# Two SwiGLU FFNs with seven block products for gate and up, a grouped down projection, and three modulation vectors made during the short convolution

## The chip, the core and the metric

One core of one Trainium2 chip runs the whole program. The metric is the device time of one execution in microseconds (us), as a median of several runs. The engines of the core work side by side, each through its own queue, strictly in the order of that queue: TensorE (PE, matrix products), VectorE (DVE, elementwise work), ScalarE (ACT, activations and copies), GpSimd (POOL, elementwise work too) and SyncE (SP, which here issues the transfers from HBM). An instruction whose inputs or whose output buffer are not ready holds up everything behind it in its own queue.

## The reference, cut to what matters

The program is two layers of a diffusion backbone on 512 tokens of 1024 channels: an attention and state-space mixer with a SwiGLU FFN behind it, then a short-convolution mixer with a second FFN, then a last normalisation. The part that the change rewrites is the FFN, and the modulation around it:

```python
D_MODEL = 1024; SEQ = 512
FFN_HIDDEN = -(-(8 * D_MODEL) // (3 * 256)) * 256      # 2816 = 22 blocks of 128

def modulate(h, shift, scale):
    return h * (1 + scale) + shift

def swiglu(h, w_gate, w_up, w_down):
    return (jax.nn.silu(h @ w_gate) * (h @ w_up)) @ w_down
```

For each layer a 1024 x 6144 matrix (`ada`) times a conditioning vector gives six modulation vectors of 1024: shift, scale and gate of the mixer (parts 0, 1, 2) and shift, scale and gate of the FFN (parts 3, 4, 5).

## The kernel before, in words

**Layout.** Activations lie transposed: 128 channels on the partitions, tokens along the free dimension. The residual stream is `xT`, eight blocks (`d` or `k`, 0 to 7) of 128 channels by 512 tokens. The tokens are handled in two halves of 256, called `e=0` and `e=1`.

**Precision.** A float32 product is made of three products of rounded operands (`mm3`, lines 113 to 118): hi times hi, hi times lo, lo times hi. So every weight block of 128x1024 is fetched into `wst` (DMA, L108), rounded by ACT into `whi` (L94), and DVE makes the rest `wlo = wst - whi` (L95). There are three buffers of each; `take` (from line 97) gives the next block of the list `plan` and starts the fetch of the ones ahead of it. Activations have a hi and a lo half in the same way (`act_hi`, `act_lo`).

**FFN before.** For each of the 22 hidden blocks `f` PE makes gate and up: two blocks of weights, eight channel blocks each, three products, 48 matmuls of 128x128 on 512 tokens. `finish` puts silu (ACT, L979), the product of gate and up (DVE, L980) and the split in hi and lo (L94, L95) behind it. All 22 hidden blocks stay in memory. Then `project` makes the down projection: for each of the eight output blocks 22 x 3 matmuls, and DVE adds the gated result to `xT` (L916). The last output block is done in two token halves, so that the norm of the first half can start while PE still works on the second.

**Norms.** The sum of squares gathers in `sq_acc` (ACT squares, POOL adds, L325). `renorm` is a job that waits on a list `due` and is called on as PE's program grows: ones-matmuls sum over the partitions (L333), nine small DVE steps make the reciprocal root (L142 to L150), a matmul spreads it over the partitions (L307), and `entry` makes the next stage's activations from it, block by block: DVE multiplies (L945), ACT or DVE applies scale and shift (L947, L949), ACT rounds (L951), DVE or POOL makes the lo half (L952). `renorm` yields 3500 columns of PE work before L333 and 8500 before L307; `flush` runs such jobs out at once. `together` (L961, L963) is the first product of a stage, made half by half.

**Modulation.** `ada_rest` fetches one 128x512 block of `ada` after the other (`ada_st`, L251), and DVE multiplies it by the conditioning vector and adds it up (L255 for the first of eight, L257 for the rest); after eight steps a transpose and a reduction follow (L260, L261). It is called in steps by `pump`. Before, part 5 of layer 0 and all six of layer 1, 7 x 16 = 112 steps, run in FFN 0 with four buffers of `ada_st`.

**Order.** The PE queue has the order in which the code is written. A scheduler orders the queues of the other engines, and the order that it chose is fixed when the program is built.

Of the kernel before, what the change touches and what calls it, by code (L numbers as in the profile page):

```python
# [7 lines left out]
F32 = mybir.dt.float32  # L8
# [31 lines left out]
NCON = CAT[-1]  # L40

# [12 lines left out]

def halves(ap):
    return ap.rearrange("p (a b) -> p a b", a=2)


class Block:
    def __init__(self, ctx, tc, t):  # L60
# [3 lines left out]
        self.plan, self.ready, self.used = [], [], 0  # L64
# [31 lines left out]

    def take(self, ahead=2):
        n = self.used
        self.used += 1
        for i in range(len(self.ready), min(n + ahead + 1, len(self.plan))):  # L100
            self.ready.append(self.weight(*self.plan[i]))
        w, self.ready[n] = self.ready[n], None
        return w

    def weight(self, src, n, extra=False):
# [3 lines left out]
        hi, lo = ((self.np if extra else self.wp).tile([P, 1024], F32R, name=x, tag=x, bufs=1 if extra else 3)  # L109
                  for x in ("whi", "wlo"))  # L110
        self.split(hi[:, :n], lo[:, :n], st[:, :n])
        return hi, lo
# [123 lines left out]
    def ada_rest(self, pool, layer, parts, acc=None, bufs=2, tag=None):  # L236
# [3 lines left out]
        for n, part in enumerate(parts):  # L240
            for j in range(2):
# [4 lines left out]
                for k in range(0, KC, step):  # L246
                    if acc is None:
# [91 lines left out]
    def hybrid(self):  # L339
# [5 lines left out]
        with tc.tile_pool(name="start", bufs=1) as sp:  # L345
# [22 lines left out]
            def weights():  # L368
                for i in range(3):
                    self.ready.append(self.weight(*self.plan[i]))  # L370
# [526 lines left out]
    def project(self, xt, m, gate, between, nk=KC, order=None, tail=1, lead=0, more=True):  # L897
# [32 lines left out]
        ws = [load(2 + more - i) for i in range(tail)]  # L930
# [6 lines left out]
    def entry(self, xt, i, j):  # L937
        nc = self.nc
        gsc, sh = self.gsc[:, i, j, :], self.mod[:, i, 3 * j, :]

        def run(e, rb):
            ts = slice(TC * e, TC * e + TC)
            for k in range(KC):
                u = self.np.tile([P, TC], F32, name="nm_u", tag="nm_u", bufs=3)
                nc.vector.tensor_tensor(u, xt[:, k, ts], rb, ALU.mult)  # L945
                if k % 2:
                    nc.vector.tensor_scalar(u, u, gsc[:, k:k + 1], sh[:, k:k + 1], ALU.mult, ALU.add)  # L947
                else:
# [193 lines left out]
```

## Time and profile before

| what | value |
|---|---|
| median of 3 runs (lowest to highest) | 1294.58 us (1290.67 to 1295.09) |
| the profiled execution: its time, its span | 1294.68 us, 1292.9 us |
| PE busy | 1241.5 us, 96% of the span |
| DVE, ACT, POOL busy | 731.7, 448.0, 182.7 us |
| the span by stages, roughly | mixer of layer 0 to 345 us, FFN 0 to 735, short convolution to 907, FFN 1 to 1281, last norm to the end |

The profiled execution lasts 1.8 us longer than its span, and lies 0.1 us above the median. A row of the trace gives a start in us, a duration, the engine, the line, the operation, and what it writes and reads; in brackets stands how long the engine had been idle before it and what ended that idle time.

### The profile page before, as it was taken

What the parts mean: (1) busy time and instruction counts of PE and PEld (TensorE: products, weight loads), DVE (VectorE), ACT (ScalarE), POOL (GpSimd) and SP (SyncE); (2) the same over time, 40 slices, a digit from 0 to 9 for tenths busy, and PEclk for the clock granted to TensorE, in tenths of its full rate; (3) what the DMA queues carried; (4) which work ended last, traced back from release to release, by engine and by line L of the source; (5) the groups of instructions that cost most, each with busy time, mean ns of one, the idle gap of its engine ahead of it and who ended that gap; (6) DMA issues with size and microseconds to landing.
All of it is one profiled execution on the core that took longest, in us unless ns stands there. A gap on an engine that the chain in (4) does not pass through costs nothing.

```text
span 1292.9 us, 15877 instructions
## 1 busy us (share of the span) xinstructions
PE 1241.5 (96%) x6086; PEld 1022.4 (79%) x6086; DVE 731.7 (57%) x1187; ACT 448.0 (35%) x675; POOL 182.7 (14%) x199
## 2 busy tenths in 40 slices
PE   5999988899999999999999999999999999999997
PEld 3887665567798888888888988888988888888886
DVE  4898899976464777788522564443643333332223
ACT  4534534455353222222222342223532222222221
POOL 3433435440220000000000110002200000000001
PEclk9998989999999999999999999999999999999998
DMA  9331453300413777777433323333133333333322
GB/s 370 125 98 49 123 166 119 98 1 1 149 63 122 229 250 241 226 235 255 123 102 90 115 67 97 98 98 114 50 114 98 98 98 98 92 96 90 92 88 66
DMA packets 54845, 158.52 MB, mean 123 GB/s; under 512 B 6000, under 2 KB 8688, under 8 KB 54512
## 3 DMA queue, kind: packets, MB, share of 16 engines
q1 hardware_dynamic: 54480, 157.20, 38.3%
q8 instruction: 48, 0.79, 0.3%
q10 hardware_dynamic: 288, 0.31, 0.1%
q14 instruction: 29, 0.24, 0.1%
HBM read 154.86 MB, written 2.10 MB: 121 GB/s over the span
## 4 chain that ended last, share of the span: by engine, by line
PE 83%; DVE 9%; issue 3%; DMA 3%; POOL 1%; ACT 1%; SPq 0%; DVEq 0%; ACTq 0%; POOLq 0%
PE psS L116 14%; PE psS L117 14%; PE psS L118 14%; PE psA L116 10%; PE psA L118 10%; PE psA L117 10%; PE psV L830 2%; DMA adaw<-ada 2%; PE psS L961 1%; DVE xtok L257 1%; DVE mx L804 1%; PE psS L822 1%; DVE wlo L95 1%; PE psS L963 1%; DMA xT<-xT 1%
## 5 line engine op out<-in xcount | busy, mean ns | idle before, releaser
L95 DVE TENSOR_TENSOR wlo<-wst,whi 128x1024 fp32r<-128x1024 f32 (+2 forms) x194 | 234.9, 1214 | 317.2 <-ACT whi L94 311.8
L94 ACT CAST whi<-wst 128x1024 fp32r<-128x1024 f32 (+2 forms) x194 | 198.4, 1026 | 549.9 <-PE psS L117 258.5
L116 PE MATMUL psS<-act_hi,whi 128*128 128x512 f32 x760 | 297.5, 391 | 1.0 <-DVE cs_a L573 0.9
L118 PE MATMUL psS<-act_hi,wlo 128*128 128x512 f32 x760 | 297.2, 391 | 0.0
L117 PE MATMUL psS<-act_lo,whi 128*128 128x512 f32 x760 | 297.2, 391 | 0.0
L118 PEld LDWEIGHTS psS<-act_hi,wlo 128*128 128x128 f32 x760 | 143.3, 189 | 30.0
L116 PEld LDWEIGHTS psS<-act_hi,whi 128*128 128x128 f32 x760 | 143.2, 188 | 29.3 <-issue 1.2
L117 PEld LDWEIGHTS psS<-act_lo,whi 128*128 128x128 f32 x760 | 143.2, 188 | 27.7
L325 POOL TENSOR_TENSOR sq_acc<-sq_acc,sq 128x512 f32<-128x512 f32 (+1 forms) x28 | 38.0, 1356 | 872.2 <-issue 645.7
L116 PE MATMUL psA<-ffn_h_hi,whi 128*128 128x512 f32 (+1 forms) x396 | 145.4, 367 | 0.0
L117 PE MATMUL psA<-ffn_h_lo,whi 128*128 128x512 f32 (+1 forms) x396 | 145.0, 366 | 0.0
L118 PE MATMUL psA<-ffn_h_hi,wlo 128*128 128x512 f32 (+1 forms) x396 | 145.0, 366 | 0.0
L257 DVE SCALAR_TENSOR_TENSOR ada_acc<-ada_st,silu_c,ada_acc 128x512 f32<-128x512 f32 x98 | 73.5, 750 | 25.5 <-DMA ada_st<-ada 24.0
L117 PEld LDWEIGHTS psA<-ffn_h_lo,whi 128*128 128x128 f32 x396 | 74.7, 189 | 12.0
L118 PEld LDWEIGHTS psA<-ffn_h_hi,wlo 128*128 128x128 f32 x396 | 74.7, 189 | 12.1
L116 PEld LDWEIGHTS psA<-ffn_h_hi,whi 128*128 128x128 f32 x396 | 74.7, 189 | 11.9
L116 PE MATMUL psA<-act_hi,whi 128*128 128x512 f32 (+1 forms) x216 | 80.0, 370 | 0.1
L118 PE MATMUL psA<-act_hi,wlo 128*128 128x512 f32 (+1 forms) x216 | 79.2, 367 | 0.8 <-DVE wlo L95 0.8
L117 PE MATMUL psA<-act_lo,whi 128*128 128x512 f32 (+1 forms) x216 | 79.6, 368 | 0.0
L916 DVE SCALAR_TENSOR_TENSOR xT<-psA,mod,xT 128x512 f32<-128x512 f32 (+1 forms) x40 | 25.6, 643 | 67.9 <-PE psA L118 67.7
L94 ACT CAST ffn_h_hi<-sg 128x512 fp32r<-128x512 f32 x44 | 27.3, 621 | 59.0 <-DVE sg L980 59.0
L118 PEld LDWEIGHTS psA<-act_hi,wlo 128*128 128x128 f32 x216 | 40.8, 189 | 8.1 <-DVE wlo L95 1.3
(297 smaller groups left out, 1810.7 us busy)
## 6 DMA issues: line engine op xcount, KB each, us to landing
wst<-w_gu SPq DMA_DIRECT2D x88, 512.0 KB, 3.6
ada_st<-ada SPq DMA_DIRECT2D x112, 256.0 KB, 4.0
wst<-w_dn SPq DMA_DIRECT2D x32, 512.0 KB, 3.5
wst<-ada SPq DMA_DIRECT2D x24, 512.0 KB, 3.8
wst<-w_sc SPq DMA_DIRECT2D x24, 512.0 KB, 3.7
adaw<-ada SPq DMA_DIRECT2D x16, 512.0 KB, 10.4
wst<-w_dn SPq DMA_DIRECT2D x16, 384.0 KB, 3.2
wst<-w_f SPq DMA_DIRECT2D x10, 512.0 KB, 3.6
```

Of the source, the lines that this page charges most:

```text
L94: nc.scalar.copy(hi, src)
L95: nc.vector.tensor_tensor(lo, src, hi.bitcast(F32), ALU.subtract)
L116: nc.tensor.matmul(out, lhsT=a[0], rhs=b[0], start=start, stop=False)
L117: nc.tensor.matmul(out, lhsT=a[0], rhs=b[1], start=False, stop=False)
L118: nc.tensor.matmul(out, lhsT=a[1], rhs=b[0], start=False, stop=stop)
L257: nc.vector.scalar_tensor_tensor(a, w[:, i], c, a, ALU.mult, ALU.add)
L325: nc.gpsimd.tensor_tensor(self.acc[:, ts], self.acc[:, ts], sq, ALU.add)
L804: nc.vector.tensor_reduce(mx[:, c:c + 1], s[:, 0:768], AX.X, ALU.max)
L822: nc.tensor.matmul(s[:, a * T:a * T + T], lhsT=kt[x][:, ks], rhs=q[x], start=(x == 0), stop=(x == 1))
L830: nc.tensor.matmul(av, lhsT=vz[:, kc, vs], rhs=e[:, a], start=(c + a == 0), stop=(c + a == CHUNKS - 1))
L916: nc.vector.scalar_tensor_tensor(xt[:, d, ts], ps, gate[:, d:d + 1], xt[:, d, ts], ALU.mult, ALU.add)
L961: nc.tensor.matmul(out, lhsT=a[:, k * P:(k + 1) * P], rhs=hi, start=(k == 0 and a is w[0]), stop=False)
```

## The change

**Gate and up by seven products.** The 2x2 block product (gate and up weights, each cut in two halves of four channel blocks, times activations cut in two channel halves and two token halves) is made with seven block products in place of eight, by sums and differences of the blocks. Each of the seven is 4 x 3 matmuls on 256 tokens: 84 matmuls for an `f`. They come in three steps per `f`: A (two products), B (three), C (two). The activation sums `t1` to `t4` are made in `combine`, part of the entry of `e=1`. The weight sums are made for each `f`: four additions of 128x512 on POOL, whose results are rounded again by ACT and DVE. The products are put together by DVE (L1175) in the tile `seven`. The lo half of the hidden block moves from DVE to POOL (L1212).

**Grouped down projection.** The hidden blocks come in groups of 5, 5, 4, 4, 4. After a group is done, its part of all eight output blocks is made and added to `xT` (L1115); only the last group of four goes through `project`.

**Modulation.** FFN 0 makes four parts (64 steps), the short convolution makes parts 3, 4, 5 of layer 1 (48 steps). `ada_st` has two buffers in place of four, and the sum is kept in the tile `u_first`.

**Weights ahead.** `take` and `release` hand over weight buffers by a count of large and small pieces; an extra buffer pair for the first block of a stage is dropped.

```diff
+SEVEN = (0, 1)
+GROUPS = ((0, 5), (5, 10), (10, 14), (14, 18), (18, 22))
+QUARTERS = 4
+
+def steps():
+    out = [("A", 0), ("A", 1), ("A", 2), None]
+    for f in range(NF):
+        out += [("A", f)] * (f > 2) + [("B", f), ("C", f)]
+        out += [("D", g) for g in range(len(GROUPS) - 1) if GROUPS[g][1] == f]
+    return out
...
+    def prepare(self, raw, i, kind, f):
+        nc, t = self.nc, self.t
+        if kind == "D":
+            return [self.down(i, d, f) for d in range(KC)]
+
+        def first():
+            st = raw[f] = self.wp.tile([P, 1024], F32, name="wst", tag="wst", bufs=3)
+            nc.sync.dma_start(out=st, in_=t["w_gu"][i, f, 0])
+            return self.rounded(self.wp, "whi", "wlo", 3, st)
+
+        def sums():
+            a1, a2 = raw[f], self.sv.tile([P, 1024], F32, name="wsu", tag="wsu", bufs=2)
+            nc.sync.dma_start(out=a2, in_=t["w_gu"][i, f, 1])
+            h = slice(0, 512), slice(512, 1024)
+            st = self.sv.tile([P, 1024], F32, name="wsa", tag="wsa", bufs=1)
+            s3, s4 = (self.sv.tile([P, 512], F32, name=x, tag=x, bufs=n) for x, n in (("ws3", 1), ("ws4", 2)))
+            nc.gpsimd.tensor_tensor(st[:, h[1]], a2[:, h[0]], a2[:, h[1]], ALU.add)
+            nc.gpsimd.tensor_tensor(st[:, h[0]], st[:, h[1]], a1[:, h[0]], ALU.subtract)
+            nc.gpsimd.tensor_tensor(s3, a1[:, h[0]], a2[:, h[0]], ALU.subtract)
+            nc.gpsimd.tensor_tensor(s4, a1[:, h[1]], st[:, h[0]], ALU.subtract)
+            raw[f] = s3, s4, a2[:, h[1]]
+            return self.rounded(self.wp, "whi", "wlo", 3, st)
+
+        def small(x):
+            return lambda: self.rounded(self.sv, "qhi", "qlo", QUARTERS, raw[f][x])
+
+        return {"A": [first], "B": [sums, small(0)], "C": [small(1), small(2)]}[kind]
...
+            if seven and e:
+                return combine(rb)
...
+        def combine(rb):
+            for k in range(4):
+                u = []
+                for x in (k, k + 4):
+                    u.append(self.np.tile([P, TC], F32, name="nm_u", tag="nm_u", bufs=3))
+                    nc.vector.tensor_tensor(u[-1], xt[:, x, TC:], rb, ALU.mult)
+                    affine(u[-1], x, nc.scalar)
+                t1, t4 = self.u0[:, k], self.u0[:, k + 4]
+                t2 = self.np.tile([P, TC], F32, name="nm_t", tag="nm_t", bufs=2)
+                nc.vector.tensor_tensor(t1, u[0], t1, ALU.subtract)
+                nc.vector.tensor_tensor(t2, u[1], t1, ALU.subtract)
+                split(self.sums(0, k), t2, nc.vector)
+                split(self.act.at(k, 1), t1, nc.vector)
+                nc.gpsimd.tensor_tensor(u[0], u[1], u[0], ALU.subtract)
+                split(self.sums(1, k), u[0], nc.gpsimd)
+                split(self.act.at(k + 4, 1), u[1], nc.vector)
+                nc.gpsimd.tensor_tensor(t4, t4, t2, ALU.subtract)
+                split(self.sums(2, k), t4, nc.gpsimd)
...
     def ffn(self, i, xt, after, bg=None):
...
+            def down(g):
+                for d in range(KC):
+                    w = self.take()
+                    ps = self.psA()
+                    lo, hi = GROUPS[g]
+                    for k in range(lo, hi):
+                        c = slice((k - lo) * P, (k - lo + 1) * P)
+                        self.mm3(ps, [a[:, c] for a in w], hid.at(k), k == lo, k == hi - 1)
+                    nc.vector.scalar_tensor_tensor(xt[:, d], ps, gate[:, d:d + 1], xt[:, d], ALU.mult, ALU.add)
+                    self.pump(1)
+
+            (self.gated_seven if i in SEVEN else self.gated)(fp, hid, down)
+            lo, hi = GROUPS[-1]
+            self.project(xt, Shifted(hid, lo), gate, after, hi - lo, lead=3 * (i in SEVEN), more=(i == 0))
...
+    def gated_seven(self, fp, hid, down):
...
+            if kind == "A":
+                p = self.get()
+                ps = self.psA((P, 2, TC))
+                cs = fp.tile([P, 4, TC], F32, name="seven", tag="seven", bufs=3)
+                product(ps[:, 0], half(p, 0), b11)
+                nc.scalar.copy(cs[:, 2], ps[:, 0])
+                product(ps[:, 1], half(p, 1), b21)
+                add(cs[:, 0], ps[:, 1], cs[:, 2])
+                live[f] = cs
+            elif kind == "B":
+                cs = live[f]
+                ps = self.psS().rearrange("p (a b) -> p a b", a=4)
+                p, q = self.get(), self.get()
+                product(ps[:, 0], half(p, 0), t2)
+                add(cs[:, 2], ps[:, 0], cs[:, 2])
+                product(ps[:, 2], q, t3)
+                add(cs[:, 3], ps[:, 2], cs[:, 2])
+                product(ps[:, 1], half(p, 1), t1)
+                z = ps[:, 1]
+                add(cs[:, 1:3], z[:, None].broadcast_to([P, 2, TC]), cs[:, 2:4])
+            else:
+                cs = live.pop(f)
+                ps = self.psA((P, 2, TC))
+                p, q = self.get(), self.get()
+                product(ps[:, 0], p, b22)
+                product(ps[:, 1], q, t4)
+                add(cs[:, 1:4:2], ps, cs[:, 1:4:2])
+                g = cs[:, 0:2]
+                nc.scalar.activation(g, g, AF.Silu)
+                for e in range(2):
+                    nc.vector.tensor_tensor(g[:, e], g[:, e], cs[:, 3 - e], ALU.mult)
+                hi, lo = hid.new(f)
+                nc.scalar.copy(hi, g)
+                nc.gpsimd.tensor_tensor(lo, g, hi.bitcast(F32), ALU.subtract)
...
+        self.flush(1)
+        for n, x in enumerate(steps()):
+            if x is None:
+                self.flush()
+            elif x[0] == "D":
+                down(x[1])
+            else:
+                step(*x)
+                if n > 3:
+                    self.pump(2 if x[1] < 6 and x[0] != "B" else 1)
...
     def shortconv(self, xt, after):
         nc, tc, t = self.nc, self.tc, self.t
         with tc.tile_pool(name="sconv", bufs=1) as fp:
             m = Pair(fp, "sconv_h", KC)
+            acc = [self.u0[:, x:x + 2].rearrange("p a b -> p (a b)") for x in (4, 6)]
+            self.queue.append(self.ada_rest(fp, 1, (3, 4, 5), acc, bufs=2, tag="ada_st"))
             self.flush(1)
...
                 self.split(*m.at(j), halves(acc))
+                self.pump(7)
+            self.pump(1000)
             self.project(xt, m, self.mod[:, 1, 2, :], after, tail=3)
...
             def late(fp):
-                yield from self.ada_rest(fp, 0, (5,), bufs=4, tag="sg")
-                yield from self.ada_rest(fp, 1, range(6), bufs=4, tag="sg")
+                acc = [self.u0[:, x:x + 2].rearrange("p a b -> p (a b)") for x in (0, 2)]
+                yield from self.ada_rest(fp, 0, (5,), acc, bufs=2, tag="ada_st")
+                yield from self.ada_rest(fp, 1, range(3), acc, bufs=2, tag="ada_st")
```

The order of instructions on the engines other than PE is the scheduler's, so the diff does not tell it. Three places are shown. In each row stand the line, the operation, the written and the read tiles and the shape.

DVE at the start of FFN 0, before: the last entry rows of `e=1`, the first product of gate and up (`sg`), and the next weight roundings.

```order
L945 TENSOR_TENSOR nm_u<-xT,psA 128x256
L952 TENSOR_TENSOR act_lo<-nm_u,act_hi 128x256
L945 TENSOR_TENSOR nm_u<-xT,psA 128x256
L947 TENSOR_SCALAR nm_u<-nm_u,gsc,mod 128x256
L952 TENSOR_TENSOR act_lo<-nm_u,act_hi 128x256
L980 TENSOR_TENSOR sg<-sg,psS 128x512
L95 TENSOR_TENSOR wlo<-wst,whi 128x1024 x2
```

The same place after the change: the end of `combine` (`nm_u`, `nm_t`, `u_first` are u, t2 and t1/t4; `tsum` holds the rounded sums), where the last row is the first addition of step B.

```order
L1052 TENSOR_TENSOR tsum_lo<-nm_t,tsum_hi 128x256
L1074 TENSOR_TENSOR u_first<-nm_u,u_first 128x256
L360 SCALAR_TENSOR_TENSOR u_first<-ada_st,silu_c,u_first 128x512
L1070 TENSOR_TENSOR nm_u<-xT,psA 128x256
L1052 TENSOR_TENSOR act_lo<-u_first,act_hi 128x256
L360 SCALAR_TENSOR_TENSOR u_first<-ada_st,silu_c,u_first 128x512
L1075 TENSOR_TENSOR nm_t<-nm_u,u_first 128x256
L1052 TENSOR_TENSOR act_lo<-nm_u,act_hi 128x256
L360 SCALAR_TENSOR_TENSOR u_first<-ada_st,silu_c,u_first 128x512
L1052 TENSOR_TENSOR tsum_lo<-nm_t,tsum_hi 128x256
L360 SCALAR_TENSOR_TENSOR u_first<-ada_st,silu_c,u_first 128x512
L1175 TENSOR_TENSOR seven<-psS,seven 128x256
```

Modulation steps (L358, L360) now stand between the steps of the entry: eight of them between the first rows of `combine` and that addition, where before there was none until the entry was over.

DVE at the start of the short convolution, before: the reciprocal root of `e=0` and the first rows of its entry.

```order
L142 TENSOR_SCALAR rs_v<-psV 128x2
L143 TENSOR_SCALAR rs_y<-rs_v 128x2
L144 TENSOR_TENSOR rs_t<-rs_y 128x2
L145 SCALAR_TENSOR_TENSOR rs_t<-rs_t,rs_v 128x2
L146 SCALAR_TENSOR_TENSOR rs_y<-rs_t,rs_y 128x2
L147 TENSOR_TENSOR rs_t<-rs_y 128x2
L148 SCALAR_TENSOR_TENSOR rs_q<-rs_t,rs_v 128x2
L149 SCALAR_TENSOR_TENSOR rs_t<-rs_q 128x2
L150 SCALAR_TENSOR_TENSOR rs_y<-rs_t,rs_y 128x2
L95 TENSOR_TENSOR wlo<-wst,whi 128x1024
L945 TENSOR_TENSOR nm_u<-xT,psA 128x256 x3
```

After, the same chain of nine and the first rows of the entry:

```order
L248 SCALAR_TENSOR_TENSOR rs_t<-rs_t,rs_v 128x2
L358 TENSOR_SCALAR u_first<-ada_st,silu_c 128x512
L249 SCALAR_TENSOR_TENSOR rs_y<-rs_t,rs_y 128x2
L250 TENSOR_TENSOR rs_t<-rs_y 128x2
L360 SCALAR_TENSOR_TENSOR u_first<-ada_st,silu_c,u_first 128x512
L251 SCALAR_TENSOR_TENSOR rs_q<-rs_t,rs_v 128x2
L252 SCALAR_TENSOR_TENSOR rs_t<-rs_q 128x2
L253 SCALAR_TENSOR_TENSOR rs_y<-rs_t,rs_y 128x2
L360 SCALAR_TENSOR_TENSOR u_first<-ada_st,silu_c,u_first 128x512
L1060 TENSOR_TENSOR nm_u<-xT,psA 128x256 x3
```

Three modulation steps stand inside the chain. In all, 23 of them (two groups of eight with their transposes and reductions, and seven more) stand ahead of the first weight rounding for the second block, `j=1`:

```order
L364 TENSOR_REDUCE ada_red<-u_first 128x16
L358 TENSOR_SCALAR u_first<-ada_st,silu_c 128x512
L360 SCALAR_TENSOR_TENSOR u_first<-ada_st,silu_c,u_first 128x512 x5
L1246 TENSOR_TENSOR u_first<-u_first,psA 128x512
L360 SCALAR_TENSOR_TENSOR u_first<-ada_st,silu_c,u_first 128x512
L180 TENSOR_TENSOR wlo<-wst,whi 128x1024
```

The transfer queue SP at the same place, before (24 weight blocks of the short convolution, then those of its output projection):

```order
L108 DMA wst<-w_sc 128x1024 x24
L108 DMA wst<-w_so 128x1024 x8
```

After, the weights and the blocks of `ada` share it:

```order
L212 DMA wst<-w_sc 128x1024 x5
L354 DMA ada_st<-ada 128x512 x2
L212 DMA wst<-w_sc 128x1024
L354 DMA ada_st<-ada 128x512 x23
L212 DMA wst<-w_sc 128x1024
```

The buffers `ada_st` of the short convolution lie in memory that FFN 0 used, and the first of these transfers waits for the last matmul of FFN 0's down projection.

## Rows read from the trace of the kernel before

**Rows 1.** The page: busy time of each engine; the chain that ended last, by engine.
```profile
PE 1241.5 (96%) x6086; PEld 1022.4 (79%) x6086; DVE 731.7 (57%) x1187; ACT 448.0 (35%) x675; POOL 182.7 (14%) x199
...
PE 83%; DVE 9%; issue 3%; DMA 3%; POOL 1%; ACT 1%; SPq 0%; DVEq 0%; ACTq 0%; POOLq 0%
```
**Rows 2.** Busy time by stretches; columns in the second row, PEclk the granted clock.
```profile
core 0: us, PE busy (x) PEld busy (x) DVE busy (x) ACT busy (x) POOL busy (x), PEclk, DMA share, GB/s
395.00:615.00 220.00, 220.00 (x973) 182.27 (x972) 162.81 (x219) 65.71 (x82) 0.00 (x0) 1.00 0.71 229
715.00:745.00 30.00, 28.39 (x224) 27.43 (x223) 17.50 (x43) 12.13 (x21) 5.61 (x5) 1.00 0.34 106
910.00:945.00 35.00, 34.45 (x249) 32.27 (x248) 25.88 (x57) 19.62 (x37) 8.12 (x10) 1.00 0.26 77
...
1284.00:1286.00 2.00, 0.91 (x4) 0.91 (x4) 0.87 (x6) 0.00 (x0) 0.00 (x0) 0.50 0.15 50
```
**Rows 3.** Timeline of PE, matmuls on 256 tokens; from the first to the last 22 steps.
```profile
718.35 0.28 PE L118 MATMUL psA<-ffn_h_hi,wlo 128*128 128x256 f32 x1
...
720.99 0.28 PE L116 MATMUL psA<-ffn_h_hi,whi 128*128 128x256 f32 x1
```
**Rows 4.** Timeline of DVE in FFN 0; then the transfers of `ada_st` from 395 to 700.
```profile
453.46 0.75 DVE L257 SCALAR_TENSOR_TENSOR ada_acc<-ada_st,silu_c,ada_acc 128x512 f32<-128x512 f32 x1 [0.21 <-DMA ada_st<-ada]
454.13 0.69 DVE L95 TENSOR_TENSOR ffn_h_lo<-sg,ffn_h_hi 128x512 fp32r<-128x512 f32 x1
454.73 0.75 DVE L257 SCALAR_TENSOR_TENSOR ada_acc<-ada_st,silu_c,ada_acc 128x512 f32<-128x512 f32 x1
457.48 0.75 DVE L257 SCALAR_TENSOR_TENSOR ada_acc<-ada_st,silu_c,ada_acc 128x512 f32<-128x512 f32 x1 [2.00 <-DMA ada_st<-ada]
...
  DMA ada_st<-ada: 24.0, 21
DMA to landing us min/median/max: 2.8/4.0/5.6
```
**Rows 5.** Timelines of DVE and POOL: alone, and beside each other.
```profile
358.09 0.73 POOL L325 TENSOR_TENSOR sq_acc<-sq_acc,sq 128x256 f32<-128x256 f32 x1 [2.15 <-ACT sq L322]
364.62 1.23 DVE L95 TENSOR_TENSOR wlo<-wst,whi 128x1024 fp32r<-128x1024 f32 x1
364.99 1.46 POOL L325 TENSOR_TENSOR sq_acc<-sq_acc,sq 128x256 f32<-128x256 f32 x1 [6.16 <-ACT sq L322]
365.76 0.70 DVE L150 SCALAR_TENSOR_TENSOR rs_y<-rs_t,rs_y 128x2 f32<-128x2 f32 x1
378.13 0.16 DVE L150 SCALAR_TENSOR_TENSOR rs_y<-rs_t,rs_y 128x2 f32<-128x2 f32 x1
719.94 1.29 POOL L325 TENSOR_TENSOR sq_acc<-sq_acc,sq 128x512 f32<-128x512 f32 x1 [13.67 <-ACT sq L322]
```
**Rows 6.** The entry of `e=1` in FFN 0 on DVE: first and last two rows.
```profile
379.17 1.08 DVE L945 TENSOR_TENSOR nm_u<-xT,psA 128x256 f32<-128x256 f32 x3 [0.87 <-PE psA L307]
...
385.11 0.41 DVE L947 TENSOR_SCALAR nm_u<-nm_u,gsc,mod 128x256 f32<-128x256 f32 x1
385.44 0.42 DVE L952 TENSOR_TENSOR act_lo<-nm_u,act_hi 128x256 fp32r<-128x256 f32 x1
```
**Rows 7.** Timeline from FFN 0 into the short convolution, DVE and PE.
```profile
726.23 0.48 DVE L916 SCALAR_TENSOR_TENSOR xT<-psA,mod,xT 128x256 f32<-128x256 f32 x1 [6.30 <-PE psA L118]
...
732.67 0.61 PE L307 MATMUL psA<-cons,rs_y 128*128 128x128 f32 x4
...
735.15 0.28 PE L118 MATMUL psA<-ffn_h_hi,wlo 128*128 128x256 f32 x1
...
755.99 0.40 PE L116 MATMUL psA<-act_hi,whi 128*128 128x512 f32 x1
```
**Rows 8.** The chain of the last microseconds.
```profile
1282.44 0.84 PE psV L333 x6
...
1285.10 1.24 PE psA L307 x4
```

More of the change, by code (lines that the diff above doesn't have):

```diff
@@ L63, in __init__ @@
         self.due = []
[L64 removed]
+        self.plan, self.used = [], 0
         for q in range(4):
@@ L71, in __init__ @@
         self.plan += [(t["w_o"][d], 1024) for d in range(KC)]
+        self.made, self.freed, self.pieces = 0, 0, []
         for i in range(2):
             if i == 1:
-                self.plan += [(t["w_sc"][j, x], 1024, j == 0 and x == 1) for j in range(KC) for x in (1, 2, 0)]
+                self.plan += [(t["w_sc"][j, x], 1024) for j in range(KC) for x in (1, 2, 0)]
                 self.plan += [(t["w_so"][d], 1024) for d in range(KC)]
-            self.plan += [(t["w_gu"][i, f, x], 1024, f + x == 0) for f in range(NF) for x in range(2)]
@@ L77, in __init__ @@
-            for d in range(KC):
-                self.plan += [(t["w_dn"][i, d, :, k:min(k + KC, NF), :], P * min(KC, NF - k)) for k in range(0, NF, KC)]
+            if i in SEVEN:
+                raw = {}
+                for x in steps():
+                    if x is not None:
+                        self.plan += self.prepare(raw, i, *x)
+            else:
+                for f in range(NF):
+                    self.plan += [(t["w_gu"][i, f, x], 1024) for x in range(2)]
+                    self.plan += [self.down(i, d, g) for g in range(len(GROUPS) - 1) if f == GROUPS[g][1]
+                                  for d in range(KC)]
@@ L95, in split, with feed @@
         nc.vector.tensor_tensor(lo, src, hi.bitcast(F32), ALU.subtract)
+    def feed(self):
+        while self.made < len(self.plan):
+            x = self.plan[self.made]
+            large = sum(1 for w, n in self.pieces[self.freed:] if n > 512)
+            if large >= 3 or len(self.pieces) - self.freed - large >= QUARTERS:
+                return
+            self.pieces.append(x() if callable(x) else self.weight(*x))
+            self.made += 1
     def take(self, ahead=2):
@@ L99, in take, with get, release, weight @@
         self.used += 1
[L100 to L105, printed above, removed]
+        self.release(n + ahead - 2)
+        return self.pieces[n][0]
+    def get(self):
+        self.feed()
+        self.used += 1
+        return self.pieces[self.used - 1][0]
+    def release(self, n):
+        for x in range(self.freed, n):
+            self.pieces[x] = None, self.pieces[x][1]
+        self.freed = max(self.freed, n)
+        self.feed()
+    def weight(self, src, n):
         nc = self.nc
@@ L368, in weights @@
             def weights():
-                for i in range(3):
-                    self.ready.append(self.weight(*self.plan[i]))
+                self.feed()
             load(ct, "ctxT")
@@ L929, in project @@
             self.pump(3)
-        ws = [load(2 + more - i) for i in range(tail)]
+        ws = [load(2 - i) for i in range(tail)]
         for e in range(2):
@@ L955, in together, with sums @@
+        return run
+    def sums(self, x, k):
+        return [a[:, x, k, :] for a in self.tsum]
     def together(self, jobs, e):
```

135 lines of the change are left out of this document (93 added, 42 removed).

## Prediction

> **What bounds the kernel now.** I read the page first: PE is busy 96% of the span and carries 83% of the chain that ended last, DVE 9% [rows 1]. Then the stretches. From 395 to 615, inside FFN 0, PE is busy without a gap, 973 matmuls in 220 us, so 0.226 us for one on 512 tokens; in the seam from FFN 0 to the short convolution it misses 1.6 us of 30, at the entry of FFN 1 0.55 us of 35 [rows 2]. So what PE does less is gained in full as long as the others keep pace, and what they make it wait is lost in full. A matmul on 256 tokens takes 2.64/22 = 0.120 us [rows 3], a little over half of 0.226: small pieces cost PE 6%.
>
> **What PE gains.** Before, an FFN makes 22 x 48 matmuls at 0.226 = 238.7 us for gate and up, and 1.0 more because the first three blocks are made half by half (72 pairs of 0.120 in place of 0.226). Down is 7 x 66 x 0.226 + 132 x 0.120 = 120.2. Together 359.9. After: 22 x 84 x 0.120 = 221.8; down in groups 432 x 0.226 = 97.6, and the last group 84 x 0.226 + 24 x 0.120 = 21.9, together 341.3. That is 18.6 us less for each FFN, 37.2 for both.
>
> **What a DVE or POOL instruction takes.** From start to start a DVE instruction takes a little less than its duration: 0.67 for a modulation step on 512 columns, 0.60 for a rounding of 512 [rows 4], 1.14 for one of 1024 [rows 5], 0.33 for one of 256 [rows 6]. POOL's addition of 256 columns is 0.73 alone, of 512 1.29; I count 0.60 and 1.15 in a row. The important reading is the pair at 364.62 and 364.99: POOL's addition of 256 columns, 0.73 alone, takes 1.46; it ends 0.7 after the DVE rounding beside it, and the two-column DVE instruction behind that takes 0.70 in place of 0.16 [rows 5]. Neither moves while the other works on two operands in SBUF. So in the changed kernel, where POOL makes four sums of 512 and one lo half for each `f`, I add POOL's time to that of the two-operand SBUF work of DVE ("exclusive time").
>
> The Trainium skill says the same of these ports (SBUF — State Buffer, "SBUF: two separate sides": an exclusive lock, not shared bandwidth), and from it warns that moving work between these two might not help (Perfetto Trace Analysis, "Optimizing Scalar/DVE Operations"). The trace agrees in the 1.46 against 0.73.
>
> **FFN 0, from the first A step to the first group's down.** Ahead of that group's first L1115 the order has on DVE: 36 modulation steps and 6 first ones, 9 roundings of 1024, 3 of 640, 14 two-operand ones of 512, 32 of 256 (these two-operand ones 56.5 us), and 25.6 us that read PSUM or one operand; 82.1 in all. On POOL 25 x 1.15 + 16 x 0.60 = 38.4. Exclusive time 56.5 + 38.4 = 94.9. PE has six `f` in this stretch and 15 matmuls, 6 x 84 x 0.120 + 3.4 = 64. The first group's down and the next five `f` don't give it back: DVE 25.0 against PE 23.7, exclusive 56.3 against 53.8. Loss 31 + 2.5 = 33. Lower bound: no exclusion, and 5 us of the lag taken up later, 82.1 - 64 - 5 = 13. Upper: halfway to strictly one after the other (120.5), 107.7 - 64 + 2.5 = 46. I stay at the exclusive sum, since that is what the rows show. It shows first at the entry: eight modulation steps stand ahead of the last t2 rounding, whereas before `e=1` took 6.7 us of DVE [rows 6] and none stood there.
>
> **The short convolution's start.** Before, the first product of the next stage starts as the projection's last matmul of `e=1` ends, at 735.27, and `j=1` follows at 755.99: 20.7 us [rows 7]. Now 23 modulation steps stand on DVE ahead of the first `j=1` rounding, and their transfers can't start before the projection ends. With two buffers, two steps take one landing and one step: landing is 2.8 at least, 4.0 in the median [rows 4], so (2.8 + 0.75 + 0.1)/2 = 1.83 or 2.4 a step. First landing 2.8, 22 more at 1.83 = 40.3, 0.7 for the last and 1.14 for the rounding: 45, less 20.7 = +24; with 2.4 it is +38. If transfers never made it wait, DVE's own work there (23 steps and two reductions 18, two entries of 6.7, two roots 3.6, rounding 1.1) is 36, +15.5. The entries fill part of the transfer waits, but the queue is in order and not all fits: I take +26, bounds 15.5 and 38. What is queued behind: three of the steps stand inside the root of `e=0`, so PE's first product waits from the start. In FFN 0 before, with four buffers, 112 steps cost DVE 24 us of waits [rows 4], hidden since nothing PE needed was behind them for long.
>
> [...]
>
> **FFN 1's entry.** `flush(1)` leaves the job of `e=1`. Its 3500 and 8500 columns are 5.6 us at 0.120 per 256, with L307 the broadcast is there 6.3 after the first A. A0 to A2 are 72 matmuls, 8.6 us; then PE needs t2. `combine` is 31 DVE instructions of 256 and 3 of 1024, 13.8 us, on POOL 17.6; exclusive 27.8. t2 of the last block needs most of DVE's list but not POOL's end; I take 19.5, about midway. 6.3 + 19.5 + 0.8 for ACT's rounding - 9.6 (8.6 and the L307 matmuls) = +17; by DVE alone +10.5, by the exclusive sum +24. Before, the same place lost 0.55 [rows 2]. What follows in FFN 1 fits: exclusive 50.1 against PE 53.8, 39.2 against 43.7 and 43.0. The 71.2 of its first stretch against 64 lie inside this loss.
>
> **The end.** Before, root and broadcast of `e=0` ran under the 66 matmuls of `e=1`; now `e=1` has 12, 1.4 us. Both roots (L333 to L307 2.7 us [rows 8]) and all multiplications follow: +3.5, bounds 2 and 5. The same cover is missing ahead of the short convolution; it is in the 26.
>
> **Clock.** Where PE has little to do, from 1284 to 1286, the granted clock is 0.50, the lower level (1.2 GHz) [rows 2]. The four stalls above (FFN 0's entry, both halves of the short convolution's, FFN 1's) restart PE so; a matmul of 0.120 would take 0.240. I take 1 us each, +4, bounds 0 and 8.
>
> **Costed at nothing.** Grouped additions (32 more L1115 of 0.75 an FFN, DVE has 15 us to spare under each group's down); the dropped extra buffer, covered by three blocks ahead and lost only where DVE is late anyway; the 25 steps left after `j=1`, 7 a block of 32 us.
>
> **Sum.** 33 + 26 + 17 + 3.5 + 4 = 83.5 lost, 37.2 gained: +46. On the profiled execution's 1294.7 (0.1 above the median) 1341 us. All lower bounds together: 13 + 15.5 + 10.5 + 2 = 41 lost, 1298. All upper: 46 + 38 + 24 + 5 + 8 = 121, 1378.
>
> **Rivals.**
> (a) *Softer losses.* POOL's sums fit into the times in which DVE waits for transfers, and landing is 2.8: about half-way between the sums and their lower bounds or below, 42 to 58 lost, 1299 to 1315. For it: POOL is idle 86% [rows 1], and a waiting DVE blocks nobody. Against it: the 1.46.
> (b) *Faster.* The lag of DVE in the two FFNs never reaches PE: three steps A ahead and three weight blocks hide it, and t2 arrives block by block, as PE uses it. Then only the short convolution and the end are left, 15.5 to 24 and 2: 1275 to 1283. It decides once the losses of the FFNs are under some 10 us together. For it: PE needs t2 only after A2. Against it: 82 us of DVE work in a stretch in which PE has 64 can't be hidden by 9 us of lead.
> (c) *Serial everywhere.* DVE and POOL hold each other also where DVE reads PSUM. Then the later runs are too long as well: 33.2 + 28.8 = 62 against 53.8, 25.8 + 23 = 48.8 against 43.7 and 43.0, 19 more for each FFN, 1379, and with the two entries serial some 1400. Against it: no row here shows a PSUM reader held by POOL. For it: no row shows the two engines working in this density either.
>
> **Chances and range.** Forecast (1315 to 1370) 0.59; (a) 0.21, of which 0.06 within 0.5% (1288 to 1301; 0.5% is about what a measurement can tell from no change); (b) 0.12; (c) 0.08. Faster 0.12, same 0.06, slower 0.82. The range from 1288 to 1370 leaves out (b) and (c).
>
> **What would show it.** After the change: matmuls on 256 tokens 0.120 apart in the FFNs and PE's busy time some 37 us lower; PE idle some 30 us in FFN 0 before 420, ended by DVE's t2 rounding, L1175 or weight roundings; DVE idle before L360 by transfers, about 1.8 a step, from 735 to 780 of the old time; the first L219 of `j=1` released by L180; PE idle about 17 us at FFN 1's entry. The prediction is wrong if PE has no idle time at the entries (b), if later groups of FFN 1 show gaps between A, B and C (c), or if modulation steps in the short convolution follow each other in under 1.3 us.

## The result and the profile after

The changed kernel takes 1548.37 us (median of 4 runs, 1541.81 to 1549.60) against 1294.41 us: ratio 1.196, interval 1.192 to 1.200. 1341 us was predicted, with a range of 1288 to 1370. The sign was right; the loss is 254 us, not 46.

The page after, busy times and the chain by engine, answers to [rows 1]:

```profile
PE 1292.6 (84%) x7420; PEld 1111.8 (72%) x7420; DVE 1032.8 (67%) x1663; ACT 562.9 (36%) x915; POOL 521.6 (34%) x443
...
PE 52%; DVE 19%; DMA 12%; issue 7%; POOL 5%; ACT 4%; SPq 0%; DVEq 0%; POOLq 0%; ACTq 0%
```

PE should have been busy 37 us less and is busy 51 us more; it stands idle for 253 us (span less busy) in place of 51. So the loss has two parts, some 202 us of idle time and 51 of longer busy time. The stretches after show the two FFN entries, and a long piece of FFN 1 far behind its entry:

```profile
core 0: us, PE busy (x) PEld busy (x) DVE busy (x) ACT busy (x) POOL busy (x), PEclk, DMA share, GB/s
371.00:420.00 49.00, 24.74 (x119) 20.62 (x120) 39.82 (x67) 17.75 (x40) 27.49 (x26) 0.67 0.22 75
1074.00:1125.00 51.00, 31.96 (x155) 27.45 (x155) 35.88 (x60) 20.84 (x46) 26.65 (x26) 0.67 0.08 27
1200.00:1500.00 300.00, 259.48 (x1668) 235.40 (x1667) 177.28 (x243) 104.82 (x154) 109.54 (x78) 0.97 0.25 79
```

The entries lose time, as forecast. The last row is the surprise: in a stretch that "fits" by the sums of the prediction, PE misses 40 us of 300 while DVE is busy 59%. What it waits for there (engine, line waited for; us in total, times, longest):

```profile
PE psS L219 <- DVE seven L1175: 32.4, 30, 2.6
PE psA L219 <- ACT seven L1184: 8.1, 16, 1.2
```

Those are all 40 us. The timeline shows one `f` of it, first DVE, then PE, then ACT:

```profile
1260.15 1.22 DVE L180 TENSOR_TENSOR wlo<-wsa,whi 128x1024 fp32r<-128x1024 f32 x1 [0.52 <-ACT whi L179]
1261.30 0.42 DVE L1175 TENSOR_TENSOR seven<-psS,seven 128x256 f32<-128x256 f32 x1
1263.49 0.42 DVE L1175 TENSOR_TENSOR seven<-psS,seven 128x256 f32<-128x256 f32 x1 [1.78 <-PE psS L221]
...
1260.26 0.28 PE L221 MATMUL psS<-tsum_hi,wlo 128*128 128x256 f32 x1
1261.77 0.39 PE L219 MATMUL psS<-tsum_hi,qhi 128*128 128x256 f32 x1 [1.23 <-DVE seven L1175]
...
1263.97 0.39 PE L219 MATMUL psS<-act_hi,whi 128*128 128x256 f32 x1 [0.52 <-DVE seven L1175]
...
1256.97 0.37 ACT L1184 COPY seven<-psA 128x256 f32<-128x256 f32 x1
1270.03 0.37 ACT L1184 COPY seven<-psA 128x256 f32<-128x256 f32 x1
```

In step B the last matmul of the product with t2 starts at 1260.26; DVE is in a weight rounding that it began at 1260.15, and adds that product up at 1261.30; only then does the product with t3 start, 1.23 us late, though it goes to another part of the tile. The third product waits in the same way (0.52) until t3's part has been read, and in step A the second product waits for ACT's copy of the first. So an `f` takes 13.06 us (from 1256.97 to 1270.03) where its 84 matmuls need 10.08. Over the whole trace:

```profile
POOL ffn_h_lo L1212 <- ACT ffn_h_hi L1211: 289.8, 34, 19.5
...
PE psS L219 <- DVE seven L1175: 102.6, 88, 6.9
...
PE psA L219 <- ACT seven L1184: 28.4, 44, 3.4
```

The first row is the largest of the view and costs nothing: POOL stands waiting for data there, and no row of PE's own waits names L1212. The other two are 131 us of PE's idle time: three stops for each of 44 `f`.

Stage lengths follow, each from one start of the last addition of `e=1` to `xT` to the next (L916 before, L1018 after; the last stage to the end of the span):

| profiled run | start of FFN 0 | FFN 0 | short conv. | FFN 1 | end |
|---|---|---|---|---|---|
| before | 370.7 | 365.5 | 180.9 | 364.4 | 11.4 |
| after | 371.0 | 483.8 | 219.7 | 455.2 | 15.9 |
| tiles apart (e1) | 375.3 | 415.3 | 219.3 | 378.8 | 16.3 |
| apart, all on DVE (e13) | 376.4 | 386.6 | 217.3 | 371.1 | 15.9 |
| eight products (e3) | 386.4 | 384.1 | 211.6 | 368.4 | 16.2 |
| grouping alone (e8) | 385.8 | 371.3 | 194.4 | 368.4 | 16.2 |
| e8 with `tail=3` (e12) | 383.9 | 373.4 | 192.0 | 368.3 | 12.6 |
| seven in FFN 1 alone (e7) | 380.8 | 370.5 | 200.5 | 381.9 | 16.3 |
| e7, all on DVE (e11) | 386.3 | 372.7 | 198.8 | 371.8 | 15.8 |

### The profile page after: what moved, and what is told of

The parts are those of the page before. It is cut to its first block, busy times and chain, and to the rows that moved or that the text cites. A ratio compares the mean times of both kernels' runs of the same rounds, so it can differ in the third digit from the quotient of the medians.

```text
span 1545.6 us, 20062 instructions
## 1 busy us (share of the span) xinstructions
PE 1292.6 (84%) x7420; PEld 1111.8 (72%) x7420; DVE 1032.8 (67%) x1663; ACT 562.9 (36%) x915; POOL 521.6 (34%) x443
## 4 chain that ended last, share of the span: by engine, by line
PE 52%; DVE 19%; DMA 12%; issue 7%; POOL 5%; ACT 4%; SPq 0%; DVEq 0%; POOLq 0%; ACTq 0%
PE psA L219 10%; PE psA L220 9%; PE psA L221 9%; PE psS L219 6%; DMA ada_st<-ada 5%; PE psS L220 5%; PE psS L221 5%; DVE seven L1175 3%; DVE wlo L180 3%; ACT whi L179 2%; DVE u_first L360 2%; DMA wst<-w_gu 2%; DMA wsu<-w_gu 2%; DVE qlo L180 2%; POOL ws L149 2%
## 5 line engine op out<-in xcount | busy, mean ns | idle before, releaser
L179 ACT CAST whi<-wst 128x1024 fp32r<-128x1024 f32 (+3 forms) x182 | 158.4, 872 | 362.6 <-PE psA L220 182.4
L180 DVE TENSOR_TENSOR wlo<-wst,whi 128x1024 fp32r<-128x1024 f32 (+3 forms) x182 | 201.6, 1109 | 27.7 <-ACT whi L179 25.6
L219 PE MATMUL psA<-act_hi,whi 128*128 128x256 f32 (+1 forms) x568 | 189.0, 333 | 30.8 <-ACT seven L1184 28.4
L221 PE MATMUL psA<-act_hi,wlo 128*128 128x256 f32 (+1 forms) x568 | 182.7, 322 | 7.6 <-DVE wlo L180 7.6
L220 PE MATMUL psA<-act_lo,whi 128*128 128x256 f32 (+1 forms) x568 | 183.5, 323 | 6.5 <-DVE act_lo L1052 5.6
L1212 POOL TENSOR_TENSOR ffn_h_lo<-seven,ffn_h_hi 128x512 fp32r<-128x512 f32 x44 | 61.8, 1405 | 289.8 <-ACT ffn_h_hi L1211 289.8
L219 PEld LDWEIGHTS psA<-act_hi,whi 128*128 128x128 f32 x568 | 111.7, 197 | 48.1 <-ACT seven L1184 37.6
L1175 DVE TENSOR_TENSOR seven<-psS,seven 128x256 f32<-128x256 f32 x132 | 67.2, 509 | 111.9 <-PE psS L221 111.1
L219 PE MATMUL psS<-act_hi,whi 128*128 128x256 f32 (+1 forms) x280 | 101.8, 364 | 38.4 <-DVE seven L1175 37.2
L220 PEld LDWEIGHTS psA<-act_lo,whi 128*128 128x128 f32 x568 | 111.8, 197 | 15.6 <-DVE act_lo L1052 7.0
L360 DVE SCALAR_TENSOR_TENSOR u_first<-ada_st,silu_c,u_first 128x512 f32<-128x512 f32 x98 | 86.2, 880 | 44.7 <-DMA ada_st<-ada 44.3
L147 POOL TENSOR_TENSOR wsa<-wsu 128x512 f32<-128x512 f32 x44 | 59.7, 1358 | 159.4 <-DVE wlo L180 68.7
L221 PE MATMUL psS<-act_hi,wlo 128*128 128x256 f32 (+1 forms) x280 | 96.7, 345 | 0.0
L220 PE MATMUL psS<-act_lo,whi 128*128 128x256 f32 (+1 forms) x280 | 96.5, 345 | 0.0
```

Of the source, the lines that this page charges most:

```text
L147: nc.gpsimd.tensor_tensor(st[:, h[1]], a2[:, h[0]], a2[:, h[1]], ALU.add)
L179: nc.scalar.copy(hi, src)
L180: nc.vector.tensor_tensor(lo, src, hi.bitcast(F32), ALU.subtract)
L219: nc.tensor.matmul(out, lhsT=a[0], rhs=b[0], start=start, stop=False)
L220: nc.tensor.matmul(out, lhsT=a[0], rhs=b[1], start=False, stop=False)
L221: nc.tensor.matmul(out, lhsT=a[1], rhs=b[0], start=False, stop=stop)
```

## The experiments

**Tiles of their own (e1, e2).** In A and B each product gets its own PSUM tile; nothing else changes.

```diff
-ps = self.psA((P, 2, TC))
+pa, pb = self.psA((P, TC)), self.psA((P, TC))
...
-ps = self.psS().rearrange("p (a b) -> p a b", a=4)
+pa, pb, z = self.psS()[:, 0:TC], self.psS()[:, 0:TC], self.psA((P, TC))
```

> Each product of steps A and B gets a PSUM tile of its own; nothing else is changed. Theory 1 (PE stands still within A and B because the next product is written into the tile that ACT or DVE still reads: 28.4 + 102.6 = 131 us of PE waits in the changed kernel's trace): these waits vanish, and the clock that fell with them comes back; 1548 falls by 131 to 200, to 1350 to 1420 us. Theory 2 (DVE and POOL together have too much to do, by their exclusion): the waits reappear in front of the weight roundings, and the time stays above 1510 us.

> Only the two products of step A get PSUM tiles of their own. Theory 1: the 28.4 us of PE waits on ACT's copy go, with some clock 28 to 50 less, 1500 to 1520 us. Theory 2: no change within 10 us.

Measured: e1 1409.76 us (ratio 1.090, 1.088 to 1.092), 139 us less; e2 (step A alone) 1513.13, 35 less. In FFN 1 from 1100 to 1380 of e1 PE misses 5.4 us of 280, all in the one row that the view of its waits has there (us, times, longest), and the clock is whole in the stretch (columns as above):

```profile
PE psA L219 <- DVE seven L1175: 5.4, 4, 1.8
```

```profile
1100.00:1380.00 280.00, 274.55 (x1842) 254.36 (x1842) 208.40 (x267) 111.75 (x174) 126.30 (x82) 1.00 0.30 93
```

Theory 1 holds: the waits are between a product and the reader of the tile that the next one is written to. They do not vanish altogether. Over the whole of e1 PE still waits 22.6 us for L1175 and 6.6 for L1184, most of it in FFN 0; in the changed kernel it is 131.

**Without seven products, without sums (e3, e4).** e3 is the changed kernel with `SEVEN = ()`. e4 leaves the four POOL additions out:

```diff
-nc.gpsimd.tensor_tensor(st[:, h[1]], a2[:, h[0]], a2[:, h[1]], ALU.add)
...
-raw[f] = s3, s4, a2[:, h[1]]
-return self.rounded(self.wp, "whi", "wlo", 3, st)
+raw[f] = a1[:, h[0]], a1[:, h[1]], a2[:, h[1]]
+return self.rounded(self.wp, "whi", "wlo", 3, a2)
```

> Both FFNs with the old eight products (48 matmuls on 512 tokens); grouped down projection and the modulation in the short convolution stay. Theory 1 and theory 2: the loss of the FFNs goes, what stays is the short convolution's start (29 us in the changed kernel) and some 0 to 30 us at FFN 0's entry: 1320 to 1355 us. Theory 3 (grouping and moved modulation are the larger part): above 1400 us.

> The four POOL additions that make the weight sums are left out in both FFNs, the unsummed weight halves are rounded in their place (so gate and up are other numbers). Theory 1: the waits within A and B stay, 10 to 40 us less from DVE being held less, 1508 to 1538 us. Theory 2: 100 us less or more, under 1450 us.

Measured: e3 1367.10, 181 less than the change, but still 72 over the kernel before, 12 over the range that either theory gave: grouping and moved modulation cost more than I had put down. e4, which computes other gate and up values, takes 1491.83, 57 less, more than theory 1 gave and less than theory 2: POOL's sums cost something of their own.

**POOL's part (e10, e9, e11, e13).** e10 is e4 on top of e1. e9, e11 and e13 give POOL's FFN work to DVE, `nc.gpsimd` to `nc.vector` in the weight sums, the hidden lo half and `combine`.

> On top of the kernel with tiles of their own (1409.8 us): the four POOL additions of the weight sums are left out in both FFNs, the unsummed weight halves are rounded in their place (gate and up are other numbers). Exclusion theory: 40 to 80 us less, 1330 to 1370 us; the eight-product kernel's 1367 is then about reached. Rival (entries and modulation hold the rest): less than 20 us less.

> On top of the kernel with t2 first (1425.0 us): all that POOL does in the FFNs (weight sums, lo half of the hidden block, sums of the entry) is done by DVE. Exclusion theory (a DVE instruction of 256 columns beside POOL's takes 0.9 in place of 0.33; POOL needs 1.15 for what DVE does in 0.61, and DVE stands still meanwhile): 30 to 80 us less, 1345 to 1395 us. Rival (POOL's work is work that DVE has no room for): DVE is the bound, 1425 us or more.

> On top of the kernel with tiles of their own (1409.8 us): POOL's work in the FFNs is done by DVE, entry and groups as in the change. If waits in the tiles and exclusion are what kept seven products behind eight, this lies under the kernel with eight products and all else alike (1367 us): 1335 to 1362 us. Rival (the entry of e=1 eats the gain of seven products in any case): 1365 us or more.

> On top of the kernel with seven products in FFN 1 alone (1356.4 us): POOL's work of FFN 1 is done by DVE. Exclusion theory: FFN 1 and its entry get 10 to 30 us shorter, 1326 to 1346 us. Rival: no change or slower, 1350 us or more.

Measured: e10 1347.79 (62 less than e1), e9 1366.66 (58 less than its base e5), e13 1365.00 (45 less than e1, but on the number of its rival: it does not get clear of the eight products' 1367), e11 1347.37 (9 less than its base e7, less than was given). Exclusion holds. The first lines of the pages of e1 and e13:

```profile
PE 1245.9 (89%) x7420; PEld 1086.9 (77%) x7420; DVE 1071.8 (76%) x1663; ACT 550.8 (39%) x915; POOL 548.6 (39%) x443
PE 1240.1 (91%) x7420; PEld 1080.7 (79%) x7420; DVE 1078.1 (79%) x1915; ACT 557.1 (41%) x915; POOL 178.3 (13%) x191
```

In e13 DVE carries 252 instructions more and is busy only 6 us longer, though the new ones take some 143 (an estimate: 220 of 512 columns at 0.60 and 32 of 256 at 0.33). So its other instructions have become shorter by nearly as much. How much of the 45 us is that, and how much that POOL was also the slower engine for the same sums, no run here separates. The sharpest rows are in FFN 1's entry of e7, DVE with and without POOL beside it:

```profile
979.32 0.41 DVE L1077 TENSOR_TENSOR nm_t<-nm_u,u_first 128x256 f32<-128x256 f32 x1
979.65 0.41 DVE L1076 TENSOR_TENSOR u_first<-nm_u,u_first 128x256 f32<-128x256 f32 x1
...
982.59 0.95 DVE L1053 TENSOR_TENSOR act_lo<-u_first,act_hi 128x256 fp32r<-128x256 f32 x1
983.46 0.94 DVE L1053 TENSOR_TENSOR act_lo<-nm_u,act_hi 128x256 fp32r<-128x256 f32 x1
...
983.22 0.91 POOL L1079 TENSOR_TENSOR nm_u<-nm_u 128x256 f32<-128x256 f32 x1
984.09 0.90 POOL L1080 TENSOR_TENSOR u_first<-u_first,nm_t 128x256 f32<-128x256 f32 x1
```

They take turns: each starts its next instruction 0.87 after its last, where DVE alone needs 0.33. This is the exclusive lock that the Trainium skill describes (SBUF — State Buffer, "SBUF: two separate sides"), and the trace agrees in the 0.87 against 0.33.

**Entry order (e5, e15).** Both stand on e1. e5 makes t2 of all blocks first in `combine`, which needs six `nm_u` and, for room, groups of 4, 4, 4, 3, 3, 4; e15 has the groups alone.

> On top of the kernel with tiles of their own (1409.8 us): the entry of e=1 makes t2 of all four block pairs, with what it needs, before the other sums are rounded (six nm_u buffers in place of three; the groups of the down projection are 4, 4, 4, 3, 3, 4 for the room). Entry theory (at each FFN's entry PE waits for t2 behind the rest of the list; 14.6 and 21.7 us of waits there, with the fallen clock some 20 and 30): 15 to 40 us less, 1370 to 1395 us. Rival (DVE and POOL have the same work in any order, PE waits for t3 or t1 in place of t2): within 8 us of 1410.

> On top of the kernel with tiles of their own (1409.8 us), only the groups are 4, 4, 4, 3, 3, 4. The kernel with t2 first was 15 us slower with this and another order: if the finer groups are the reason, 1418 to 1430 us; if the order is, 1405 to 1414 us.

Measured: e5 1424.99, 15 more than e1, against what was expected; e15 1418.50, 9 more. So the finer groups cost some 9, and the other order is no help (6 more, with two runs each that lie 4 to 6 us apart). In e5's entry to FFN 1 the first t2 rounding on DVE starts at 1042.36, behind an `act_lo` rounding at 1038.15: the scheduler did not keep t2 ahead, and POOL's sums still took turns with DVE. That an order exists that shortens the entry is not excluded.

**Four buffers (e6).** On top of e1, `bufs=2` becomes `bufs=4` for the modulation in the short convolution.

> On top of the kernel with tiles of their own (1409.8 us): ada_st has four buffers in place of two in the short convolution, the 23 modulation steps ahead of the first rounding of j=1 stay. Transfer theory (two buffers make a step take a landing and a step for two): the stage, 219 us against 181.6 before, gets 12 to 25 us shorter, 1385 to 1398 us. Rival (DVE's own work in that order sets it): within 6 us of 1410.

Measured: 1401.70, 8 less, between the two theories; its two runs lie 11 us apart (1396.03 and 1407.37), so the time alone decides nothing. In the short convolution the transfer waits fall from the first row (e1) to the second (us, times), and the stage only from 219.3 to 212.8:

```profile
  DMA ada_st<-ada: 26.1, 26
...
  DMA ada_st<-ada: 3.7, 4
```

22 us of waits taken away bring 6.5, and the end of the first rounding for `j=1` comes 45.7 after the start of the stage in place of 49.8. So the rival was nearer: the transfer waits are the smaller part. That DVE's own work in that order sets the rest is likely, but not shown.

**One FFN, and grouping alone (e7, e8, e12).** e7 is e5 (tiles apart, t2 first, six groups) with seven products in FFN 1 alone and the modulation in FFN 0 with four buffers. e8 has neither seven products nor moved modulation. e12 is e8 with `tail=3` in the last group's `project`.

> FFN 0 with eight products and the modulation as before (all 112 steps there, four buffers), nothing of it in the short convolution; FFN 1 with seven products in tiles of their own and the entry with t2 first. If the causes are rightly named: FFN 1 was 16 us longer than before with tiles of their own, the entry gives 10 to 25 back, the end costs 4.5: 1285 to 1305 us. Rival (DVE and POOL can't carry seven products at PE's pace): above 1310 us.

> Eight products and the modulation as before (all in FFN 0, four buffers); only the grouped down projection and its weight supply are left of the change. If the 72 us that the kernel without seven products loses are the moved and two-buffered modulation: 1294 to 1305 us, from the longer end alone. Rival (the groups cost): above 1325 us.

> On top of the kernel with grouping alone (1338.5 us): the last group's projection leaves its last three output blocks, not one, to the halves by token, so e=1 has 36 matmuls (4.3 us) behind the start of the norm of e=0 in place of 12 (1.4 us). Cover theory (the norm of e=0 and its broadcast have no matmuls to lie under at the seam to the short convolution and at the end): 4 to 10 us less, 1328 to 1335 us. Rival (the seam's loss is weights or entry work on DVE): within 3 us of 1338.

Measured: e7 1356.35 (ratio 1.051), outside what was expected and where its rival put it, partly for what e8 shows: grouping alone is 1338.50 (1.036, 1.034 to 1.037). The rival's reason holds in part: FFN 1 of e7 takes 381.9, and with POOL's work on DVE (e11) 371.8. By stages grouping alone costs 15 before FFN 0 (32 of FFN 0's modulation steps, L358 and L360, run before that mark; in the changed kernel the first starts at 396), 6 in FFN 0, 13.5 in the short convolution, 4 in FFN 1, 5 at the end. The 15 thus need not be grouping's own price. The seam of e8, L410 of both halves with only the ones-matmuls of the norm (L436) between them:

```profile
761.07 1.22 PE L410 MATMUL psA<-cons,rs_y 128*128 128x128 f32 x4 [1.83 <-DVE rs_y L253]
767.94 1.23 PE L410 MATMUL psA<-cons,rs_y 128*128 128x128 f32 x4 [4.16 <-DVE rs_y L253]
```

e12 is 1334.10 (1.030 to 1.034), 4 less, at the upper edge of what was expected: the end shrinks from 16.2 to 12.6. The seam gains nothing. The short convolution is 2.3 shorter, but FFN 0 is 2.1 longer; together they take 565.7 in e8 and 565.5 in e12. There L410 still waits 3.62 and 4.15:

```profile
759.64 1.09 PE L410 MATMUL psA<-cons,rs_y 128*128 128x128 f32 x4 [3.62 <-DVE rs_y L253]
766.38 1.22 PE L410 MATMUL psA<-cons,rs_y 128*128 128x128 f32 x4 [4.15 <-DVE rs_y L253]
```

So missing cover is shown for the end and not for the seam, whose loss was not taken apart.

**The best of it (e14).** e13 with four buffers and `tail=3`.

> The same, and four ada_st buffers in the short convolution and three output blocks of the last group by token halves: some 4 to 8 us less from the seams and 5 to 10 from the transfers, 1320 to 1350 us; still above the kernel before, since each entry still makes PE wait. Rival: within 4 us of the kernel without these two.

Measured: 1357.44 (1.050, 1.047 to 1.052), 8 less than e13, 7 over its range and far above the kernel before. No version here beats that one.

## Why the prediction was wrong

**The step that failed** is "What follows in FFN 1 fits: exclusive 50.1 against PE 53.8, 39.2 against 43.7 and 43.0", and with it "what PE does less is gained in full as long as the others keep pace". I compared what each engine has to do in a stretch. I did not follow one `f` from product to reader to product. The code has it in plain sight: `product(ps[:, 0])`, a read of `ps[:, 0]`, `product(ps[:, 1])` in the same tile. No sum of busy times shows such a chain: DVE was 41% idle where PE waited for it. Three stops of together 2.2 us idle, and 0.8 more in running out and starting again, make 13.06 out of 10.08; 44 times 2.98 is 131. That the view's waits come to 131 as well is in part chance: they hold no running out, but longer stops at the entries. e1 gives 139 back, in its profile 94 of PE's idle time and 47 of its busy time for the same 7420 matmuls. In the kernel before, a tile's products are all done when it is read, so its trace had no such row.

The Trainium skill has a rule that bears on step A (PSUM — Partial Sum Buffer, "PSUM bank collisions raise a hardware error"): a write of TensorE and a read by ACT or DVE must be kept apart by bank, not by address. Both products of A lie in one tile of 2 KiB, one bank's size, so that wait could have been named from it. The page does not cover the two waits in B, 102.6 of the 131 us: each product there waits for the read of a part in the other 2 KiB of its tile. A shared tile is enough for the wait; whether it is guarded as a whole or for another reason, no run here tells. e2 took A's wait away alone (35 us), e1 all of them.

**Beyond the stops.** Even e1 is 115 us over the kernel before, not 46. By the stages of the profiled runs it is 49.8 over in FFN 0 (14 forecast), 38.5 in the short convolution (26), 14.4 in FFN 1 (a gain of 2), and 9.5 before FFN 0 and at the end (3.5).

**PE's gain (37).** Right for the matmuls, 0.120 apart again (two of the changed kernel start at 1262.82 and 1262.94), but seen as time only far from the entries, and only with tiles apart: there an `f` of e13 takes 10.07 (copies L1184 at 1184.42 and 1194.49), where 48 matmuls at 0.226 take 10.8. What the seven win there the entries lose (FFN 1's in e13, columns as above):

```profile
979.00:1029.00 50.00, 35.72 (x210) 32.60 (x211) 41.76 (x95) 24.92 (x52) 4.00 (x4) 0.73 0.10 32
```

The whole times of e13 (1365.0) and of the eight products in e3 (1367.1) look level, but are no clean pair: in e3, 22 modulation steps run before FFN 0, which starts 10 us later than in e13. FFN 1 has no modulation, and there seven products are the longer ones: 371.1 against 368.4, and 371.8 (e11, with finer groups) against 368.4 (e8).

**FFN 1's entry (+17).** In e1, where POOL still has its part, FFN 1 is 10.4 us longer than with eight products (e3), against a gain of 17.9 (18.6 less 0.7 that the groups' matmuls bring in both). That is 28 lost, 5.4 of them behind the entry: some 23, near the upper bound of 24. In e13 it is 21, within bounds that were made for another split of the work.

**FFN 0's first stretch (+33).** The mechanism is shown, the size was too small. The sign given for it, PE idle some 30 us before 420, measured 24.3 (371 to 420). But the stage in e1 is 49.8 over before, so with the gain of 18.6 some 68 are lost, over the upper bound of 46. PE misses 24 us of the first 50 and 27 in the rest of the stage, for which the forecast had 2.5; from 425 to 560 DVE is busy 127 us of 135. Without POOL's sums (e10) 37 of the 68 go.

**Exclusion.** Right as a mechanism; also that FFN 1 carries POOL's sums behind its entry (5.4 us of 280 missed in e1). Without the sums e1 falls by 62: by stages 37 in FFN 0, where DVE has the modulation as well, and 14 in FFN 1 (its stages 377.9 and 364.8). POOL's price was low: additions of 512 columns start 1.25 to 1.36 apart in the changed kernel (L1212 to L149 at 1230.95, L147 to L148 at 1234.71), not the 1.15 that I counted. (In the pair of [rows 5] POOL ends 0.6 behind the rounding, not 0.7; nothing hangs on it.)

**The short convolution (+26).** 38.8 by stages, just over the upper bound of 38. 13.5 of it comes from grouping, 17 from the modulation (e3 against e8), 8 only with seven products. The stops are inside the norm, as described, but the long one is the other half's: the root of `e=0` holds two modulation steps (the third of the listed order stands behind it, after L253) and L410 waits 3.87; L410 of `e=1` waits 14.20 for a root with five of them, a transpose and a reduction in it.

```profile
860.86 1.22 PE L410 MATMUL psA<-cons,rs_y 128*128 128x128 f32 x4 [3.87 <-DVE rs_y L253]
877.78 1.22 PE L410 MATMUL psA<-cons,rs_y 128*128 128x128 f32 x4 [14.20 <-DVE rs_y L253]
```

Of the transfers of `ada_st` in the changed kernel its view says:

```profile
DMA to landing us min/median/max: 2.7/2.9/7.6
```

The median of 2.9 with two buffers was near the 2.8 that I chose, but by e6 the transfers account for the smaller part, and even with four buffers the rounding for `j=1` ends 45.7 after the start of the stage, where DVE's own work alone was put at 36.

**The end (+3.5)** measured 4.5. **The clock (+4)** was far too little: the granted clock is 0.67 on average over both entries, a mix of the lower level (0.5) and the full one, and 0.933 over the run against 0.989. Behind PE's waits in FFN 0's entry, from 410 to 420, it is 0.50 and two matmuls on 256 tokens start at 414.35 and 414.56, 0.21 apart in place of 0.12. How much of the 254 it is by itself was not measured; the 47 us of busy time in e1's gain contain it.

**Costed at nothing: grouping.** Wrong. In e8 it is some 28 us beside the 15 before FFN 0. 4.8 of the 28 are the end, which had a price, and part of the 13.5 at the short convolution lay in the 26; the 6 in FFN 0 and the 4 in FFN 1 had none.

**The rivals.** (a) and (b) are refuted. (c) came nearest (1379 to 1400), still 148 short, and its sign, gaps between A, B and C in later groups of FFN 1, is what the trace shows; but not its cause, since the gaps went with the tiles, not with POOL.

## What to carry to other kernels

Sums of engine time against the bound engine say only whether a pace is possible; before trusting them, follow one round of the loop through every hand-over, and ask of each write of PE which reader must have left that tile. Where a product is cut into pieces that are read one by one, give each piece a tile of its own. And when work is moved to POOL beside a DVE that works on two SBUF operands, count both times as one. When a stage is compared between two versions, look at both sides of its marks: what the short convolution of e12 wins, its FFN 0 loses, and part of e3's modulation lies ahead of its FFN 0.

## What the runs showed of the hardware

DVE and POOL take turns so strictly that a DVE instruction of 256 columns on two SBUF operands goes from 0.33 to 0.87 from start to start when POOL has a queue of its own (e7), for as long as both have work. A matmul on 256 tokens comes every 0.120 us at the full granted clock and every 0.21 at 0.50. Blocks of 256 KB landed in 2.9 us in the median with two buffers, against 4.0 with four in the kernel before [rows 4]; in the short convolution, where nothing but the number of buffers differs, in 3.0 with two (e1) and 3.3 with four (e6).
